# A gap of 96 bytes and one column buffer fewer, ahead of the weight buffers in on-chip memory

## The chip, the cores and the metric

The kernel runs as one program on one core of a Trainium2 chip. The metric is the device time of one execution in microseconds (us): 1457.18 us is the median of three runs, which lie between 1455.75 and 1457.39 us.

## The reference

One sequence of 256 tokens of width 1024 passes seven sublayers in float32: a gated feed-forward (SwiGLU, inner width 2816), an mLSTM mixer, two feed-forwards, a Mamba-2 mixer, a feed-forward, and a hybrid layer (attention of 8 heads beside a gated short convolution). Around each of the first six stands

```
hmod = rms_norm(x, g_pre) * (1 + scale) + shift
y    = rms_norm(fn(hmod), g_post)
x    = x + weight * gate * y
```

`shift`, `scale` and `gate` come from a vector `c` through large matrices (`ada_w`, `w_ada_2`). Nearly all the time is matrix products of the 256 tokens with about 330 MB of float32 weights, each read once.

## The kernel before

**Split weights.** TensorE multiplies in a shorter float32 form (fp32r), so each operand is split into a high part and the rest: `hi` is the weight rounded to fp32r, `lo` is `raw - hi`. A product then takes three matmuls: high by high, high by low, low by high. The activations are split in the same way (`XH`, `XL` for the normalised input; `gh`, `gl` for the inner activations of a feed-forward and the mixers; `AH`, `AL`, `CH`, `CL`, `MH`, `ML` in the hybrid layer).

**The stream.** Class `Stream` (lines 111 to 262) loads the weights in units of 128 rows by 1024 floats, 4096 bytes in each row: a load by SyncE into one of nine `raw` buffers, a cast to `hi` on ScalarE (ACT) or VectorE (DVE), and a subtraction to `lo` on DVE. There are six `hi` and six `lo` buffers. Units that multiply the vector `c` go from `raw` straight into the sums `accC` and `accG` (`mac`, line 366).

**Two roles in a matmul.** TensorE (PE) loads one operand as weights in its array (the stationary operand, 128 columns here) and streams the other through it (the moving operand). In `proj_t` (line 681) the stationary operand is a 128-column piece of `hi` or `lo`, and `XH` or `XL` moves with 256 columns (all the tokens). In `unit_b` and `unit_wide` (lines 709 and 755) it is the other way about: 128 tokens of `XH`, `XL`, `gh` or `gl` are stationary, and 512 columns of `hi` or `lo` move. The profile names the moving operand first: `pa<-XH,hi` moves `XH`, `py<-hi,gh` moves `hi`. The last unit or two of a feed-forward, and the last of the mLSTM, have buffers of their own in the stage's pool (`house`, line 124; `hix`, `lox` in the profile), but are used in the same way and beside the others.

**Order.** The order on every engine is fixed when the program is built, by the `Stream` and a small model of the engines' clocks (`Clock`, `Meter`). It doesn't look at addresses.

**Places in memory.** Pools are laid out one behind another in each row (partition) of the on-chip memory, and each tile begins at the next multiple of 32 bytes. The pool `cst` stands first; in it lie `X`, `XH`, `XL`, small constants, the bf16 scratch `junk`, then the column buffers `AB` (shift and scale of a sublayer as columns, 64 bytes each, line 408) and two buffers `G`. Behind it come `raw`, `hi`, `lo`, `scr`, the small tiles, `accC` and `accG`, and the pools that the stages open and close. In bytes modulo 128, before the change:

| tiles | start |
|---|---|
| `X`, `XH`, `XL` | 0 |
| `G`, all `raw`, `hi`, `lo`, `scr` | 32 |
| `accC`, `accG` | 64 |
| tiles of the first feed-forward (`gf`, `gh`, `gl`, `hix`, `lox`) | 32 |
| `gh`, `gl`, `hix`, `lox` of the mLSTM | 0 |
| the same in the other three feed-forwards; the Mamba-2 tiles; `AH`, `AL`, `CH`, `CL`, `MH`, `ML` | 64 |

The pieces that matmuls take from these tiles begin at multiples of 512 bytes within them, so they have the same value modulo 128.

Of the kernel before, what the change touches and what calls it, by code (L numbers as in the profile page):

```python
# [10 lines left out]
F32 = mybir.dt.float32  # L11
# [254 lines left out]
def tile_blocks(ctx: ExitStack, tc, x, c, ada_w, ada_b, norm_pre, norm_post, ffn_w1, ffn_w3, ffn_w2,  # L266
# [8 lines left out]
    cst = ctx.enter_context(tc.tile_pool(name="cst", bufs=1))  # L275
# [22 lines left out]
    isel = cst.tile([128, 32], F32R, name="isel")  # L298
    cs = cst.tile([128, 16], F32, name="cs")
    junk = cst.tile([128, 512], mybir.dt.bfloat16, name="junk")  # L300

    def pa(shape):
        return psum.tile(shape, F32, name="pa")
# [94 lines left out]
    Gs, ABs = {}, {}  # L398
# [4 lines left out]
    def cols_set(n, p, hs=(0, 1)):  # L403

        v = lambda t: t.rearrange("p (i h) -> p i h", h=2)
        g = colT[:, 16 + 8 * n:24 + 8 * n] if n < 6 else colT[:, 64:72]
        if n not in ABs:
            ABs[n] = cst.tile([128, 16], F32, name="AB", bufs=3)
        for j, h in enumerate(hs):
            if h:  # L410
                V.scalar_tensor_tensor(v(ABs[n][:, 0:8]), p[:, 4 * j:4 * j + 4], 1.0, v(g), op0=OP.add, op1=OP.mult)
            else:
                V.tensor_copy(v(ABs[n][:, 8:16]), p[:, 4 * j:4 * j + 4])

    def ada_cols(n, hs):

        p = side[0]([128, 512])
        us = st.take(len(hs))
        for i in range(8 * len(hs)):
            h, j = i // 8, 4 * (i // 8) + i % 4  # L420
            w = st.get(us[h])[i // 4 % 2]
            T.matmul(p[0:8, 0:256], pick[:, 7 - j:15 - j], w[:, 0, 256 * (i % 4):256 * (i % 4) + 256],
                     start=(i == 0), stop=(i == 8 * len(hs) - 1))
            if i % 8 == 7:
                st.done(us[h])
        r = small.tile([8, 256], F32, name="rows", bufs=1)
        A.copy(r, p[0:8, 0:256])

        def columns():
            q = side[0]([128, 512])  # L430
            for i in range(2):
                T.transpose(q[:, 8 * i:8 * i + 8], r[:, 128 * i:128 * i + 128], ident[:8, :8])
            cols_set(n, q[:, 0:16].rearrange("p (h i) -> p i h", h=2), hs)

        later(3, lambda: safe.append(columns))
# [1177 lines left out]
    with tc.tile_pool(name="pst", bufs=1, space=PSUM) as pst:  # L1613
# [53 lines left out]
        for j in range(16):  # L1667
            cols_sum(p, j)
        pieces("A", 2)
        cols_set(0, p[:, 0:16].rearrange("p (i h) -> p i h", h=2))  # L1670
        affine(tr, 0, 0, "A", True)
        affine(tr, 0, 1, "V")
# [76 lines left out]
```

## Time and profile before

| what | value |
|---|---|
| median of three runs | 1457.18 us |
| the profiled execution | 1456.93 us |
| its span, first to last instruction | 1455.1 us |
| TensorE busy | 1414.0 us, 9482 matmuls |
| VectorE busy | 1225.1 us |
| ScalarE busy | 631.6 us |
| loads and stores | 338.86 MB, mean 233 GB/s |

The span stands 1.8 us below the time of its own execution. Matmuls overlap one another: the duration of one (some 280 ns with 256 columns) is longer than the distance from its start to the next start (some 118 ns), and it is that distance that adds up to the time. It is read from the starts of a row of matmuls, or as the length of a piece of the chain of waits over its count.

### The profile page before, as it was taken

To read this page: it belongs to the slowest core of one execution; us is meant where nothing else is said; L and a number is where in the kernel's file an instruction comes from. 1 tells how busy PE (TensorE), PEld (TensorE's weight loads), DVE (VectorE), ACT (ScalarE), POOL (GpSimd) and SP (SyncE) were. 2 spreads that over 40 slices of the span, in tenths; PEclk is the share of its full clock that TensorE was granted. 3 is DMA by queue.
4 is the path that set the end of the run, shared out by engine and by line. 5 is a ranking of instruction groups with operands and counts; after the bars stand their busy time and mean duration, and the time that the engine had idled before them with its cause. 6 is when DMAs were issued, how large, how long until landed. Compare 5 with 4: busy or idle time off the path is not lost.

```text
span 1455.1 us, 24247 instructions
## 1 busy us (share of the span) xinstructions
PE 1414.0 (97%) x9482; PEld 1281.3 (88%) x9482; DVE 1225.1 (84%) x1755; ACT 631.6 (43%) x1139; POOL 37.9 (3%) x52
## 2 busy tenths in 40 slices
PE   4999999999999999999999999999999999999997
PEld 2899988977999988999889977789998799999996
DVE  7889878978989889888899999887888866879675
ACT  4433336367433354233465876552235613523112
POOL 2000000000000000000100000000000000000000
PEclk9999999999999999999999999999999999999999
DMA  9889955864998867879656444567888664456550
GB/s 376 311 303 357 325 187 194 270 236 158 338 331 314 321 213 250 309 271 319 216 177 174 131 131 131 159 231 231 308 300 286 223 188 131 147 190 201 174 174 30
DMA packets 144011, 338.86 MB, mean 233 GB/s; under 512 B 11496, under 2 KB 23320, under 8 KB 143768
## 3 DMA queue, kind: packets, MB, share of 16 engines
q1 hardware_dynamic: 142088, 332.25, 67.0%
q0 software_dynamic: 1552, 4.81, 0.9%
q8 instruction: 74, 1.21, 0.3%
q14 instruction: 41, 0.34, 0.1%
q10 hardware_dynamic: 256, 0.25, 0.0%
HBM read 334.64 MB, written 2.62 MB: 232 GB/s over the span
## 4 chain that ended last, share of the span: by engine, by line
PE 85%; DVE 7%; ACT 5%; issue 2%; DMA 1%; POOL 0%; ACTq 0%; DVEq 0%; POOLq 0%
PE pa L107 65%; PE py L107 19%; DVE scr L107 2%; ACT junk L107 2%; DVE lo L107 1%; PE cp L107 1%; ACT scr L107 1%; DMA raw<-in_ffn_w_dram 1%; DVE X L107 0%; ACT hi L107 0%; DVE accC L107 0%; ACT L107 0%; DVE XS L107 0%; ACT ss L107 0%; DVE E L107 0%
## 5 line engine op out<-in xcount | busy, mean ns | idle before, releaser
L107 DVE TENSOR_TENSOR lo<-raw,hi 128x1024 fp32r<-128x1024 f32 x450 | 542.2, 1222 | 41.9 <-ACT hi L107 29.3
L107 PE MATMUL pa<-XH,hi 128*128 128x256 f32 x2000 | 566.8, 283 | 1.0 <-ACT tmp L107 1.0
L107 PE MATMUL pa<-XL,hi 128*128 128x256 f32 x2000 | 561.8, 281 | 0.0
L107 PE MATMUL pa<-XH,lo 128*128 128x256 f32 x2000 | 561.7, 281 | 0.0
L107 PEld LDWEIGHTS pa<-XH,hi 128*128 128x128 f32 x2000 | 376.8, 188 | 3.3 <-ACT tmp L107 1.2
L107 PEld LDWEIGHTS pa<-XL,hi 128*128 128x128 f32 x2000 | 377.0, 188 | 1.5 <-issue 0.5
L107 PEld LDWEIGHTS pa<-XH,lo 128*128 128x128 f32 x2000 | 376.8, 188 | 0.0
L107 ACT CAST hi<-raw 128x1024 fp32r<-128x1024 f32 x270 | 275.9, 1050 | 175.1 <-PE pa L107 104.5
L107 DVE SCALAR_TENSOR_TENSOR accC<-raw,cs,accC 128x1024 f32<-128x1024 f32 x112 | 140.2, 1279 | 7.2 <-DMA accC<-in_ada_b_dram 7.1
L107 DVE CAST hi<-raw 128x1024 fp32r<-128x1024 f32 x180 | 124.1, 690 | 16.5 <-PE pa L107 16.2
L107 PE MATMUL pa<-hi,XH 128*128 128x512 f32 x320 | 125.9, 407 | 2.0 <-ACT junk L107 1.1
L107 PE MATMUL pa<-lo,XH 128*128 128x512 f32 x304 | 118.9, 398 | 0.0
L107 PE MATMUL py<-lo,gh 128*128 128x512 f32 x352 | 111.8, 396 | 0.0
L107 PE MATMUL py<-hi,gh 128*128 128x512 f32 x352 | 111.3, 397 | 0.0
L107 PE MATMUL py<-hi,gl 128*128 128x512 f32 x352 | 110.6, 395 | 0.0
L107 PE MATMUL pa<-hi,XL 128*128 128x512 f32 x320 | 96.5, 402 | 2.6 <-DVE ss L107 1.2
L107 ACT ACTIVATE sil<-pa 128x256 f32<-128x256 f32 (+1 forms) x80 | 32.3, 405 | 131.4 <-PE pa L107 131.4
L107 ACT CAST gh<-gf 128x256 fp32r<-128x256 f32 x72 | 28.0, 407 | 125.0 <-DVE gf L107 125.0
L107 PEld LDWEIGHTS py<-lo,gh 128*128 128x128 f32 x352 | 66.2, 188 | 15.7
L107 PEld LDWEIGHTS py<-hi,gl 128*128 128x128 f32 x352 | 66.2, 188 | 15.6
L107 DVE TENSOR_TENSOR gf<-pa,sil 128x256 f32<-128x256 f32 (+1 forms) x80 | 34.3, 447 | 50.7 <-PE pa L107 50.6
L107 PEld LDWEIGHTS py<-hi,gh 128*128 128x128 f32 x352 | 64.5, 188 | 13.9
(306 smaller groups left out, 1568.8 us busy)
## 6 DMA issues: line engine op xcount, KB each, us to landing
raw<-in_ffn_w_dram SPq DMA_DIRECT2D x264, 512.0 KB, 5.4
raw<-in_ada_w_dram SPq DMA_DIRECT2D x144, 512.0 KB, 5.3
raw<-in_w_in_dram SPq DMA_DIRECT2D x80, 512.0 KB, 3.9
raw<-in_mb_w_in_dram SPq DMA_DIRECT2D x41, 512.0 KB, 3.8
raw<-in_ml_w_in_dram SPq DMA_DIRECT2D x25, 512.0 KB, 5.1
raw<-in_w_ada_dram SPq DMA_DIRECT2D x24, 512.0 KB, 5.3
raw<-in_mb_w_out_dram SPq DMA_DIRECT2D x16, 512.0 KB, 4.2
raw<-in_ml_w_out_dram SPq DMA_DIRECT2D x8, 512.0 KB, 5.9
```

What stands on the lines that cost most here:

```text
L107: return fn(out, *args, **kw)
```

## The change

The pool `cst` gets a tile of 24 floats (96 bytes) between `junk` and the column buffers, which nothing reads or writes, and there are two column buffers instead of three (128 bytes instead of 192). All that lies behind begins 32 bytes later. Modulo 128, `G`, `raw`, `hi`, `lo` and `scr` go from 32 to 64, the tiles of the first feed-forward from 32 to 64, those of the mLSTM from 0 to 32, and all that stood at 64 goes to 96. `X`, `XH` and `XL` stay at 0. No instruction is added, removed or moved on any engine, and every instruction waits for the same semaphore values as before.

```
     junk = cst.tile([128, 512], mybir.dt.bfloat16, name="junk")
+    cst.tile([128, 24], F32, name="gap")
...
         if n not in ABs:
-            ABs[n] = cst.tile([128, 16], F32, name="AB", bufs=3)
+            ABs[n] = cst.tile([128, 16], F32, name="AB", bufs=2)
```

## Rows read from the trace of the kernel before

**Rows 1.** The page, parts 1 and 2: busy time; slices of the span
```profile
PE 1414.0 (97%) x9482; PEld 1281.3 (88%) x9482; DVE 1225.1 (84%) x1755; ACT 631.6 (43%) x1139; POOL 37.9 (3%) x52
...
PEclk9999999999999999999999999999999999999999
```
**Rows 2.** The page, part 4: the chain that ended last
```profile
PE 85%; DVE 7%; ACT 5%; issue 2%; DMA 1%; POOL 0%; ACTq 0%; DVEq 0%; POOLq 0%
PE pa L107 65%; PE py L107 19%; DVE scr L107 2%; ACT junk L107 2%; DVE lo L107 1%; PE cp L107 1%; ACT scr L107 1%; DMA raw<-in_ffn_w_dram 1%; DVE X L107 0%; ACT hi L107 0%; DVE accC L107 0%; ACT L107 0%; DVE XS L107 0%; ACT ss L107 0%; DVE E L107 0%
```
**Rows 3.** Busy time by stretches (us) in the second feed-forward; PEclk, DMA share, GB/s
```profile
393.51:404.71 11.20, 11.20 (x51) 9.02 (x50) 11.20 (x15) 5.70 (x7) 0.00 (x0) 1.00 0.80 276
404.71:427.43 22.72, 22.72 (x194) 22.72 (x193) 17.69 (x18) 6.85 (x11) 1.98 (x3) 1.00 0.97 368
```
**Rows 4.** Chain of waits in order of time: start us, us, what
```profile
393.51 11.20 PE py L107 x48
404.71 22.72 PE pa L107 x192
...
1273.48 151.31 PE pa L107 x1284
```
**Rows 5.** Groups of instructions by line and form: PE
```profile
L107 PE MATMUL pa<-XH,hi 128*128 128x256 f32 x2000 | 566.8, 283 | 1.0 <-ACT tmp L107 1.0
...
L107 PE MATMUL pa<-hi,XH 128*128 128x512 f32 x320 | 125.9, 407 | 2.0 <-ACT junk L107 1.1 <-ACT XH L107 0.9
...
L107 PE MATMUL pa<-lo,XH 128*128 128x512 f32 x304 | 118.9, 398 | 0.0
L107 PE MATMUL py<-lo,gh 128*128 128x512 f32 x352 | 111.8, 396 | 0.0
...
L107 PE MATMUL pa<-AH,hi 128*128 128x256 f32 x64 | 17.9, 279 | 0.0
...
L107 PE MATMUL py<-lo,MH 128*128 128x512 f32 x32 | 10.9, 395 | 0.0
```
**Rows 6.** Timeline of PE, end of second feed-forward: start us, us, instruction
```profile
530.51 0.39 PE L107 MATMUL py<-hix,gh 128*128 128x512 f32 x1
...
531.87 0.63 PE L107 MATMUL py<-hi,gh 128*128 128x512 f32 x2
...
533.27 0.63 PE L107 MATMUL py<-hi,gh 128*128 128x512 f32 x2
```
**Rows 7.** Timeline of PE, end of the mLSTM
```profile
335.79 0.39 PE L107 MATMUL py<-hix,gh 128*128 128x512 f32 x1
...
337.16 0.63 PE L107 MATMUL py<-hi,gh 128*128 128x512 f32 x2
...
338.56 0.39 PE L107 MATMUL py<-hi,gh 128*128 128x512 f32 x1
```
**Rows 8.** Timeline of PE, end of the first feed-forward
```profile
222.09 0.39 PE L107 MATMUL py<-hix,gh 128*128 128x512 f32 x1
...
223.48 0.62 PE L107 MATMUL py<-hi,gh 128*128 128x512 f32 x2
...
224.86 0.64 PE L107 MATMUL py<-hi,gh 128*128 128x512 f32 x2
```
**Rows 9.** Timeline of PE in the hybrid layer
```profile
1369.00 0.28 PE L107 MATMUL pa<-CH,hi 128*128 128x256 f32 x1
...
1371.80 0.28 PE L107 MATMUL pa<-CH,hi 128*128 128x256 f32 x1
```
**Rows 10.** Timeline of PE where 8 columns are stationary
```profile
204.86 0.62 PE L107 MATMUL pa<-hi,pick 128*8 128x256 f32 x4
...
206.24 0.63 PE L107 MATMUL pa<-lo,pick 128*8 128x256 f32 x4
```
**Rows 11.** Groups of DVE, 66 to 212 us and 375 to 540 us
```profile
L107 DVE TENSOR_TENSOR gl<-gf,gh 128x256 fp32r<-128x256 f32 x16 | 5.9, 417 | 0.0
...
L107 DVE TENSOR_TENSOR gl<-gf,gh 128x256 fp32r<-128x256 f32 x18 | 6.8, 419 | 0.1
```

## What the change will do: the prediction

> **What bounds the kernel now.** I read the page's busy times first: PE is busy 1414.0 of 1455.1 us, DVE 1225.1 [rows 1]. A busy PE might still wait for others, so the chain of waits comes next: PE has 85% of it, 65% in matmuls that write `pa` and 19% in those that write `py` [rows 2]. The busy time by stretches shows the same inside a feed-forward: PE has no gap in 393.51 to 427.43 us, at full granted clock, while DVE is busy 11.20 of 11.20 us in the `py` stretch and 17.69 of 22.72 us in the `pa` stretch [rows 3]. So the time is the number of matmuls times the distance between their starts, and DVE, with 85% of that group, is the next bound.
>
> The distances come from the chain. 48 `py` matmuls with 512 columns take 11.20 us, 233.3 ns each; 192 `pa` matmuls with 256 columns take 22.72 us, 118.3 ns each [rows 4]. They hold on to these values through the whole kernel.
>
> **Whether a start matters.** The change issues no instruction and shifts addresses only, so I looked for places where before already has the same matmul at another start. The ends of the stages are such places: there `hix` and `lox` move instead of `hi` and `lo`, with the same shape, the same stationary tiles, one right behind the other.
> - Second feed-forward: six matmuls with `hix`, `lox` at 64 modulo 128 take 530.51 to 531.87, 1.36 us, 226.7 ns each. The next six, with `hi`, `lo` at 32, take 1.40 us, 233.3 ns each [rows 6].
> - mLSTM: `hix`, `lox` at 0 take 1.37 us for six, the next six at 32 take 1.40 us [rows 7].
> - First feed-forward: here `hix`, `lox` stand at 32 as `hi` and `lo` do, and the two sixes take 1.39 and 1.38 us [rows 8].
>
> So a moving operand of 512 columns that begins at a multiple of 64 goes 6.6 ns faster (2.8%) than one at 32 past it, and where both stand at 32 the difference is gone. The stationary tile matters less: `gh` at 64, 0 and 32 under the same moving `hi` gives 233.3, 233.3 and 230 ns [rows 6 to 8].
>
> The page "SBUF — State Buffer" of the Trainium skill (section Door 1) says that consecutive accesses within 16-byte lines run at full bandwidth; by it a start at 32 is as good as one at 64, and the time would stay at 1457. The rows speak against it: 226.7 beside 233.3 ns. That rule is rival D.
>
> **The sum.** All against the profiled execution, 1456.93 us, which is 0.25 us below the median.
> 1. Moving `hi` and `lo` go from 32 to 64. Their matmuls: 320 of `hi` by `XH`, as many by `XL`, 304 of `lo` by `XH`, three groups of 352 by `gh` and `gl`, three of 32 by `MH` and `ML` [rows 5], and 140 in smaller groups: 2236 by 6.6 ns, 14.8 us less.
> 2. `hix` and `lox` go the other way in four stages (64 to 96, 0 to 32): 84 matmuls by 6.6 ns, 0.5 us more; the 12 of the first feed-forward gain 0.1.
> 3. `AH`, `AL`, `CH`, `CL` move with 256 columns in six groups of 64 [rows 5], and go from 64 to 96. No row shows 256 columns at both starts. Bounds: nothing, or 6.6 ns as with 512. I take half, 3.3 ns for half the columns: 384 by 3.3 ns, 1.3 us more (0 to 2.5). The 96 matmuls that move `hi` by `pick` gain 0.3 by the same measure.
> 4. The 6000 matmuls that move `XH` or `XL` (three groups of 2000 [rows 5]) keep their moving start at 0; only their stationary `hi` or `lo` goes from 32 to 64. I take zero, by the rows on `gh` above. The other ends: half of 226.7 ns is 113.3, so at best 5.0 ns less each, 30 us; at worst 3.3 ns more each, 20 us.
> 5. DVE and ACT read and write the same tiles. `gl` from `gf` and `gh` takes 417 ns where all three stand at 32 and 419 ns where they stand at 64 [rows 11]: zero.
> 6. The loads write `raw` at 64 instead of 32. DMA holds 1% of the chain [rows 2], 15 us; a packet 3% slower or faster would move it by 0.5 us. Zero.
> 7. Two column buffers: a buffer is rewritten two sublayers after its last reading, and no wait differs from before. Zero.
>
> Lines 1 to 3 give 13.3 us. PE's own idle time is 41 us of the span, and in the `py` stretches DVE has no slack [rows 3], so some of the gain is lost again in waits for `lo`; I pass on nine tenths: 12.0 us. 1456.93 - 12.0 = 1444.9, forecast **1445**. Its own range is 1437 to 1451: if DVE held back all of the gain in the matmuls by `gh` and `gl` (1056 by 6.6 ns, 7.0 us), 1451 would be left; if the stationary start were worth 1.4 ns to the 6000 (8.4 us, by 0.9), 1437.
>
> Of step 4 there is more to say, since it is the largest unknown. 118.3 ns is 5 ns over half of 226.7, with a moving operand that begins at 0. Something costs these 5 ns, and the stationary `hi` at 32 is one candidate. The other is the load of the weights itself, which with 256 columns has half the time to hide in. With only 8 stationary columns (`pick`) and a moving `hi` at 32, twelve matmuls take 1.38 us, 115 ns [rows 10]: less than 118.3 in spite of the worse start, so the weight load costs something as such. And `CH` at 64 over the same `hi` at 32 takes 2.80 us for 24, 116.7 ns [rows 9], so a mere shift of the moving start by 64 is worth 1.6 ns.
>
> The page "TensorE: Matmul & The Clock Gate" of the Trainium skill (part 2, the weight-load step) gives PE two independent read ports, one for the moving operand and one for the weights, so that a load takes nothing from the running matmul. By it the stationary start can't matter and step 4 is zero; that hangs together with the `gh` rows, but not with `pick`, whose small load is quicker.
>
> **The rivals.**
> - B: any operand off a multiple of 64, moving or stationary, costs the slow pace. Then the 6000 fall to 113.3 ns: 30.0 us less. In exchange the matmuls by `gh`, `gl`, `MH`, `ML` outside the first feed-forward (about 900, stationary now at 96 or 32) gain nothing: 5.9 us back. 13.3 + 30.0 - 5.9 = 37.4, of which I pass on eight tenths since DVE is then near its limit all through: 1427. For it: the unexplained 5 ns. Against it: the `gh` rows.
> - B': the 6000 fall to the 116.7 ns that `CH` shows: 9.8 us more, (13.3 + 9.8) by 0.9 is 21 us: 1436. For it: the offset between the two operands becomes 64 in size where it was 32. Against: nothing says that the offset is what distinguishes `CH`.
> - C, slower: with `XH` at 0 and `hi` at 64 both reads of a 256-column matmul begin on a multiple of 64 and get into each other's way, 3.3 ns each time (the upper end of step 4): 20 us by 0.9 more, 1456.9 - 12.0 + 18 = 1463. The place is every `proj_t` in the feed-forwards and the hybrid layer; it outweighs the gain from 2.0 ns a matmul up (12.0 us over 6000). For it: 118.3 and 116.7 ns show that the pairing of starts has some effect. Against: `hix` by `gh`, at 64 and 64 and at 0 and 0, is the fastest pair in the trace.
> - D, no change: `hix` is fast for another reason than its start, for example because it is alone in its buffers while `hi` rotates through six. Then 1457. Against it: the first feed-forward, whose `hix` is just as alone and as slow as `hi` [rows 8].
>
> **Chances and range.** Forecast 0.55, B' 0.14, B 0.12, C 0.10, D 0.09. What a measurement of this kernel can tell from no change is about 0.2%, 2.9 us. Faster: forecast, B' and B, 0.81; same: D, 0.09; slower: C, 0.10. The range leaves out C and the lower half of B: 1425 to 1458.
>
> **What the profile after would show.** Right: a piece of 48 `py` matmuls in the chain takes 10.9 us instead of 11.20, and one of 192 `pa` still 22.7 us; `hix` is now slower than `hi` at the end of the second feed-forward; DVE's groups keep their means; DVE's share of the span rises to 85%, with more waits of PE for `lo`. B shows 21.8 us for the 192, with `py` hardly faster outside the first feed-forward; B' 22.4; C over 23.1. The forecast is wrong in its ground if the 48 `py` still take 11.20 us, and wrong in its passing on if they take 10.9 and the span falls by less than 8 us.

## The result, and the profile after

The changed kernel takes 1434.2 us (median of 4 runs, 1431.8 to 1435.8); the kernel before took 1457.2 us beside it. The ratio is 0.9845, with a 95% interval of 0.9832 to 0.9858: 23 us faster. The forecast was 1445 us. The profiled execution after took 1431.77 us, with a span of 1430.0 us. All times leave out three executions, one of them the profiled one of the kernel with a gap of 160 bytes (whose trace is therefore not used), that took between 2.3 and 6.4 ms.

The page after, busy times and the chain of waits by engine (before: [rows 1, 2]):

```profile
PE 1388.1 (97%) x9482; PEld 1258.6 (88%) x9482; DVE 1223.5 (86%) x1755; ACT 631.6 (44%) x1139; POOL 37.9 (3%) x52
...
PE 82%; DVE 10%; ACT 4%; issue 2%; DMA 1%; ACTq 0%; SPq 0%; DVEq 0%
```
PE is busy 25.9 us less, the span is 25.1 us shorter, DVE's work is the same within 2 us. So PE's matmuls became quicker and nearly all of it was passed on. Which matmuls, the chain of waits in the second feed-forward tells (start us, us, what; before: [rows 4]):

```profile
389.17 11.19 PE py L107 x48
400.36 21.77 PE pa L107 x192
```
48 `py` took 11.20 us and take 11.19. 192 `pa` took 22.72 us and take 21.77: from 118.3 to 113.4 ns each. That is the reverse of what I had forecast. The groups of PE say the same for the whole span (busy, mean ns of one; before: [rows 5]):

```profile
L107 PE MATMUL pa<-XH,hi 128*128 128x256 f32 x2000 | 559.0, 280 | 1.3 <-ACT tmp L107 1.1 <-DVE y L107 0.3
...
L107 PE MATMUL pa<-hi,XH 128*128 128x512 f32 x320 | 124.8, 403 | 2.0 <-ACT junk L107 1.1 <-ACT XH L107 0.9
...
L107 PE MATMUL pa<-lo,XH 128*128 128x512 f32 x304 | 117.8, 394 | 0.0
L107 PE MATMUL py<-lo,gh 128*128 128x512 f32 x352 | 111.8, 396 | 0.0
...
L107 PE MATMUL pa<-AH,hi 128*128 128x256 f32 x64 | 17.9, 279 | 0.0
```
Every pair of `XH` or `XL` with `hi` or `lo` is quicker, whichever of the two moves (means of 283, 407 and 398 ns became 280, 403 and 394). `hi` and `lo` over `gh` (396) and `AH` over `hi` (279) are as before. DVE has its old load in both stretches (us; busy PE, PEld, DVE, ...; before: [rows 3]):

```profile
389.17:400.36 11.19, 11.19 (x50) 9.02 (x50) 11.19 (x15) 5.70 (x7) 0.00 (x0) 1.00 0.83 288
400.36:422.13 21.77, 21.77 (x193) 21.77 (x193) 17.70 (x18) 6.81 (x11) 1.98 (x3) 1.00 1.01 388
```

The trace holds one more thing. In the first feed-forward the `pa` stretches stayed near the old pace (chain of waits after; before they took 22.72 us):

```profile
129.46 22.61 PE pa L107 x192
152.07 11.13 PE py L107 x48
163.20 22.61 PE pa L107 x192
```
22.61 us for 192 is 117.8 ns each, and every matmul of such a stretch has this pace. Over the whole span about 80% of the `XH`, `XL` matmuls run at 113 to 114 ns and the rest near 118, in whole stretches but for the first few matmuls of some; the mean is 114.3 ns.

### The profile page after: what moved, and what is told of

Its sections match the earlier page's. It is cut to its first block, busy times and chain, and to the rows that moved or that the text cites. A ratio compares the mean times of both kernels' runs of the same rounds, so it can differ in the third digit from the quotient of the medians.

```text
span 1430.0 us, 24247 instructions
## 1 busy us (share of the span) xinstructions
PE 1388.1 (97%) x9482; PEld 1258.6 (88%) x9482; DVE 1223.5 (86%) x1755; ACT 631.6 (44%) x1139; POOL 37.9 (3%) x52
## 4 chain that ended last, share of the span: by engine, by line
PE 82%; DVE 10%; ACT 4%; issue 2%; DMA 1%; ACTq 0%; SPq 0%; DVEq 0%
PE pa L107 61%; PE py L107 19%; DVE scr L107 3%; DVE lo L107 3%; ACT junk L107 2%; PE cp L107 1%; ACT scr L107 1%; PE pb L107 1%; DMA oh<-in_consts_dram 1%; DVE hi L107 1%; DVE XS L107 1%; DMA raw<-in_mb_w_in_dram 1%; DVE X L107 0%; DVE E L107 0%; ACT L107 0%
## 5 line engine op out<-in xcount | busy, mean ns | idle before, releaser
L107 DVE TENSOR_TENSOR lo<-raw,hi 128x1024 fp32r<-128x1024 f32 x450 | 542.1, 1222 | 36.2 <-ACT hi L107 23.7
L107 PE MATMUL pa<-XH,hi 128*128 128x256 f32 x2000 | 559.0, 280 | 1.3 <-ACT tmp L107 1.1
L107 PE MATMUL pa<-XL,hi 128*128 128x256 f32 x2000 | 554.0, 277 | 0.0
L107 PE MATMUL pa<-XH,lo 128*128 128x256 f32 x2000 | 554.0, 277 | 0.0
L107 PE MATMUL pa<-lo,XH 128*128 128x512 f32 x304 | 117.8, 394 | 0.0
L107 PEld LDWEIGHTS pa<-hi,XL 128*128 128x128 f32 x320 | 59.2, 189 | 18.3 <-DVE XL L107 5.0
```

Source lines behind the costliest of these rows:

```text
L107: return fn(out, *args, **kw)
```

## The experiments

All kernels are the kernel before with other gaps of unused bytes or, once, with two column buffers; none issues another instruction. Below, D is where the moving tile of a matmul begins minus where its stationary tile begins, modulo 256. The slices that one matmul reads begin at multiples of 512 bytes within their tiles, so D is the same for all matmuls of a pair of tiles. Addresses are those that the build assigned; paces are mean distances from one matmul's start to the next in the traces.

**The change halved: the gap alone.**
```diff
+    cst.tile([128, 8], F32, name="gap")      # behind junk; AB keeps bufs=3
```


> One half of the change alone: three column buffers as before, and a gap of 32 bytes, so that hi, lo and all behind them stand where the whole change puts them (hi, lo at 64 modulo 128, XH, XL at 0). Theory R (what counts is the difference of the two starts, moving minus stationary, modulo 64; where it is 0 a matmul is fast, where it is 32 it is slow): same as with the whole change, 1434 us (1431 to 1437), 192 pa matmuls in about 21.8 us, 48 py in 11.20. Theory B (what counts is each operand's own start: off a multiple of 64 is slow): the same, since no start differs. Rival N (the third column buffer itself takes part in it, by the waits for its release): between 1440 and 1457.

Measured: 1431.2 us, ratio 0.9829 (0.9816 to 0.9843), beside 0.9845 (0.9832 to 0.9858) for the whole change. The second feed-forward reads as after the change:
```profile
399.02 21.77 PE pa L107 x192
```
The gap alone gives the whole gain: the two intervals overlap, and no effect of the number of column buffers shows beyond the bytes that it frees. N falls.

**The buffers alone.**
```diff
-            ABs[n] = cst.tile([128, 16], F32, name="AB", bufs=3)
+            ABs[n] = cst.tile([128, 16], F32, name="AB", bufs=2)
```


> The other half alone: two column buffers and no gap. hi, lo move by 64 bytes, from 32 to 96 modulo 128; the difference to XH, XL stays 32 modulo 64. R and B: as before, 1457 us (1454 to 1460), 192 pa in 22.7 us, 48 py in 11.20. N: some of the gain, 1434 to 1450. If the start modulo 128 and not modulo 64 counted, 192 pa would leave 22.7 us.

Measured: 1448.8 us, ratio 0.9951 (0.9937 to 0.9965): faster by 8 us, where R and B had no change.
```profile
390.64 11.20 PE py L107 x48
401.84 22.40 PE pa L107 x192
```
A shift of `hi`, and of all that lies behind it, by 64 bytes took the 192 from 22.72 to 22.40 us. Whatever the rule is, it doesn't repeat after 64 bytes.

**Both operands off a multiple of 64.**
```diff
+    cst.tile([128, 8], F32, name="gapx")     # ahead of X
+    cst.tile([128, 8], F32, name="gap")      # behind junk
```


> X, XH, XL (and the small constants behind them) moved by 32 bytes, hi and lo by 64 in all: XH, XL at 32 and hi, lo at 96 modulo 128, so neither begins at a multiple of 64, and their difference is 0 modulo 64. The stage tiles (gh, AH, CH, MH) stay at 32 from hi. R: 192 pa in about 21.8 us, 256-column matmuls of XH by hi at 113 to 115 ns, py unchanged at 11.20 for 48; 1434 us (1430 to 1438). B: both operands are now off, so all stay slow: 118.3 ns or more, 22.7 us for 192, 1457 us or more.

Measured: 1432.0 us, ratio 0.9836 (0.9820 to 0.9852).
```profile
398.95 21.77 PE pa L107 x192
```
With `XH` at 32 and `hi` at 96 the pace is that of 0 and 64, to the hundredth of a us. Moving both operands by 32 leaves the pace as it is: the difference counts, and not either start. B, and the ground of my forecast with it, falls.

**The stage tiles moved by 32.**
```diff
+    small.tile([128, 8], F32, name="gaps", bufs=1)   # ahead of accs
+    rc.tile([128, 8], F32, name="gapr")              # first in the pool "start"
```


> The kernel before with the stage tiles (gh, gl, hix, AH, CH, MH and the rest) moved by 32 bytes and nothing else: hi, lo stay at 32 modulo 128, gh comes to 96 or 32, so their difference becomes 0 modulo 64 outside the first feed-forward (where it is 0 before and after). XH by hi stays at 32 apart. R: 48 py in 10.9 us (226.7 ns each) instead of 11.20, AH and CH over hi at 113.4 instead of 116.7 ns, 192 pa unchanged at 22.7; about 900 by 6.6 ns and 384 by 3.3 ns are 7.2 us, of which DVE, full in the py stretches, may hold back some: 1451 us (1449 to 1456). B: gh, AH, CH now stand off a multiple of 64, so nothing is gained and some may be lost: 1457 to 1461 us, py 11.20 or more.

Measured: 1455.7 us, ratio 0.9995 (0.9986 to 1.0004): nothing. But the trace has two answers. The first feed-forward in the chain of the kernel before:
```profile
120.47 11.14 PE py L107 x48
```
The first and the second feed-forward in this kernel (the second before: [rows 4]):
```profile
120.58 10.99 PE py L107 x48
...
392.93 11.19 PE py L107 x48
```
In the second, where D became 192 (a multiple of 64, as R asks), `py` stayed. In the first, where D went from 128 to 64, it fell from 11.14 to 10.99. R falls here: being a multiple of 64 apart isn't enough. A few pairs apart (listed under the table below), the paces so far fit one table by D modulo 256, and D of 64 is also what `hi` by `XH` has after the change. That was the next theory, R256.

**`hi` further on, three times.** Only the size of the gap behind `junk` changes (96, 160, 224 bytes: 24, 40, 56 elements), and the stage tiles move along.
```diff
+    cst.tile([128, 24], F32, name="gap")     # 40 and 56 in the other two
```


> Three column buffers and a gap of 96 bytes: hi, lo at 0 modulo 128, as XH and XL; the stage tiles move along with hi. Theory R (the difference of the two starts modulo 64 decides, here 0): as the whole change, 1434 us (1430 to 1438), 192 pa in 21.8 us. Theory R256 (the difference counts modulo 256; D is the moving start minus the stationary one): for hi by XH D is 128, which in the first feed-forward and the mLSTM (hi by gh) went with 232.3 ns; for XH by hi D is 128 too, with 256 columns in no run so far, so between 113.4 and 118.3 ns: 1432 to 1457 us.

> Three column buffers and a gap of 160 bytes: hi, lo begin at 64 modulo 128 and XH, XL at 0, word for word as after the change, but 128 bytes further on; the stage tiles move along. R, and any rule on starts modulo 128: 1434 us (1430 to 1438), 192 pa in 21.8 us. R256: D is 64 for XH by hi, where AH and CH over hi took 117.8 ns, and 192 for hi by XH, where hi by gh took 233.2 ns: 192 pa in 22.6 us, 1453 us (1449 to 1458).

> Three column buffers and a gap of 224 bytes: hi, lo and XH, XL begin at the same place modulo 256 (D is 0 both ways); the stage tiles move along with hi. R256: D of 0 went with 226.7 ns for hix by gh, so hi by XH takes 226.7 to 229 ns, and XH by hi half of it, 113.4 ns: 1432 us (1428 to 1436). R: hi at 96 and XH at 0 modulo 128 are 32 apart modulo 64? No: the start of hi is 128 modulo 256, as XH's, so the difference is 0 modulo 64 too and R gives 1434 as well. A theory by which the two operands, beginning at the same place, get in each other's way would give 1457 or more.

Measured: 96 bytes 1459.5 us, ratio 1.0023 (1.0013 to 1.0034); 160 bytes 1450.2, 0.9958 (0.9942 to 0.9975); 224 bytes 1462.5, 1.0042 (1.0027 to 1.0057). The time with 160 bytes is that of three runs (1448.9 to 1451.1). The chain of the other two, 96 and then 224:
```profile
405.37 22.78 PE pa L107 x192
```
```profile
404.90 23.02 PE pa L107 x192
```
The kernel with 160 bytes is the plainest: `hi` at 64 modulo 128 and `XH` at 0, as the change's own description has it, and 16 us slower than the change. Modulo 64 or 128 nothing holds; R is done with. Of R256 the form stands, two of its sizes don't: at D of 128 `XH` by `hi` takes 118.9 ns in the mean, just above the upper bound, and at D of 0 it takes 119.9 where I expected 113.4, half of what 512 columns take. With 512 columns D of 0 is quick all the same (228.0 ns for `hi` by `XH`). The two widths have tables of their own.

**`gh` level with `hi`.**
```diff
+    cst.tile([128, 8], F32, name="gap")
+    small.tile([128, 56], F32, name="gaps", bufs=1)
+    rc.tile([128, 40], F32, name="gapr")
```


> The gap of 32 bytes (hi, XH as after the change) and the stage tiles 224 bytes further (160 more in the first feed-forward), so that gh, gl, AH, CH and MH begin at the same place modulo 256 as hi (D is 0; in the mLSTM 192). R256: 48 py in 10.9 to 11.0 us outside the mLSTM (226.7 to 229 ns each) instead of 11.20, AH and CH over hi 113.4 instead of 116.7 ns; about 950 by 5 ns and 384 by 3.3 ns are 6 us, of which DVE, full in the py stretches, may hold back up to all: 1428 us (1424 to 1433). R: the same, since D is 0 modulo 64. If py stays at 11.20 us, something other than the offset of the two tiles sets it.

Measured: 1434.9 us, ratio 0.9858 (0.9841 to 0.9874): no better than the change, and above the expected 1424 to 1433.
```profile
387.65 10.92 PE py L107 x48
398.57 22.61 PE pa L107 x192
```
`py` gained what R256 gave it, 11.19 to 10.92 us. But the `pa` stretch behind it, with its D unchanged, now runs at 117.8 ns. So at D of 192 `XH` by `hi` has two paces, and a stretch keeps to one. Over the span 46% are quick here, 80% after the change. `AH` and `CH` over `hi`, now at D of 0, went from 116.7 to 119.8 ns where I expected 113.4; `XH` by `hi` has 119.9 at that D (224 bytes).

**`gh` 64 bytes off `hi`.** After the change the stretches right behind `hi` by `XH` (D 64) and behind `py` at D of 224 were quick, those behind `py` at 128 slow.
```diff
+    cst.tile([128, 8], F32, name="gap")
+    small.tile([128, 40], F32, name="gaps", bufs=1)
+    rc.tile([128, 40], F32, name="gapr")
```


> As e9_py0, but the stage tiles 64 bytes less far (gaps of 32 ahead of the weights, 160 ahead of the stage tiles, 160 in the first feed-forward), so that hi begins 64 past gh, gl, AH, CH and MH modulo 256, as it does past XH (D is 64 for hi by gh, 192 for AH and CH over hi; 0 in the mLSTM). Theory R256 with modes (the pace follows D; at D of 192 XH by hi runs a whole stretch at either 113.4 or 117.7 ns, by what preceded it: fast behind D of 64 or 224, slow behind 0 or 128): 48 py in 11.0 us (229 ns each, 1036 by 4 ns is 4 us), AH and CH over hi at 113.4 to 114 ns (1.1 us), and the 432 XH matmuls behind py in the first feed-forward at 113.4 instead of 117.7 (1.8 us), so 1432.5 less 7: 1426 us (1423 to 1430). Rival (the slow mode comes with any faster py, since PE then outruns what prepares its operands): the slow share of XH by hi rises as in e9_py0, 1432 to 1436 us.

Measured: 1426.7 us, ratio 0.9797 (0.9783 to 0.9812).
```profile
387.06 10.98 PE py L107 x48
398.05 21.79 PE pa L107 x192
```
`py` and `pa` are quick together, and `CH` and `CL` over `hi` and `lo`, at D of 192, take twelve rounds of three matmuls in 4.08 us, 113.3 ns each (timeline of PE in the hybrid layer):
```profile
1339.78 0.28 PE L107 MATMUL pa<-CH,hi 128*128 128x256 f32 x1
...
1343.86 0.28 PE L107 MATMUL pa<-CH,hi 128*128 128x256 f32 x1
```
The rival (a faster `py` as such brings the slow pace) falls. One part failed: in the first feed-forward the slow pace stayed, behind `py` at D of 64 (chain of waits):
```profile
116.92 11.01 PE py L107 x48
127.93 22.61 PE pa L107 x192
```

**The two offsets left, to close the table** (gaps of 64 and 128 bytes).
```diff
+    cst.tile([128, 16], F32, name="gap")     # 32 in the other
```


> Three column buffers and a gap of 64 bytes: hi stands 96 past XH modulo 256, D is 96 for hi by XH and 160 for XH by hi (with 256 columns in no run so far); the stage tiles move along. R256: hi by XH 233.3 ns as E shows at 96; XH by hi open between 113.4 and 119.9 ns, the rows on both sides (128: 118.9, 192: 114.3 in the mean) make 117 likely: 1450 us (1430 to 1462). A rule modulo 64 (32 apart): 1457, 118.3 ns.

> Three column buffers and a gap of 128 bytes: hi begins at 32 modulo 128 exactly as in the kernel before, only 128 bytes further; the stage tiles move along. D is 160 for hi by XH (234.1 ns where hi by gh has it) and 96 for XH by hi (256 columns, in no run so far; its neighbours 64 and 128 took 117.8 and 118.9 ns). R256: 1457 us (1452 to 1463), with a mean for XH by hi that differs from 118.3. A rule modulo 64 or 128: exactly as before, 1457 us, 118.3 and 233.3 ns.

Measured: 64 bytes 1457.8 us, ratio 1.0009 (1.0000 to 1.0019); 128 bytes 1465.5, 1.0068 (1.0052 to 1.0085). The chain of the one and of the other:
```profile
403.34 22.79 PE pa L107 x192
```
```profile
405.17 23.04 PE pa L107 x192
```
For the first I had taken 117 ns as likely, and it is 118.4 in the mean. The second puts `hi` where it was modulo 128, and is 10 us slower than before: no rule modulo 128 allows that. It is also above the 1452 to 1463 that I gave, since `XH` by `hi` at D of 96 takes 120.0 ns.

**What sets the pace that is kept.** The kernel with `gh` 64 off, without its gap in the first feed-forward:
```diff
-    rc.tile([128, 40], F32, name="gapr")
```


> As e10_py64 without the extra 160 bytes in the first feed-forward: there hi begins 224 past gh modulo 256 instead of 64 past it (D of 224 for hi by gh, as in the second to fifth feed-forward after the change). It asks what leaves XH by hi at the slow 117.7 ns in the first feed-forward (two stretches of 192 and one of 48). If it is the D of the py matmuls ahead of them: 224 was followed by the fast 113.4 ns in nine stretches out of nine after the change, so the three stretches come to 21.8 us for 192; 432 by 4.3 ns less, 250 py by 4.2 ns more, 1425.9 us. If it is the place (the first feed-forward, whatever the offset): 117.7 ns stays, 22.6 us for 192, and py at 233.3 ns costs 1.0 us: 1427.7 us.

Measured: 1425.0 us, ratio 0.9787 (0.9773 to 0.9800), the lowest median of all, though its interval overlaps that of the kernel before it. The decision lies in the trace of the first feed-forward:
```profile
118.65 11.19 PE py L107 x48
129.84 21.78 PE pa L107 x192
```
`py` is slower there and all three stretches behind it are quick, at the same place in the program where they were slow. So the place doesn't decide; what differs ahead of these stretches is the D of `py`, and with it the pace that a stretch takes. `py` at D of 224 led to the quick one in 12 stretches of 12 that followed without a pause (9 after the change, 3 here), at D of 0 and 128 to the slow one in 15 of 15 (12 with `gh` level, 3 after the change). At D of 64 it led to either (quick in 9 of 12 with three gaps), and after a pause, or right behind the few matmuls by `pick`, both occur; what decides there is open.

The paces in the traces, in ns per matmul. The moving tile is named first; a value is the mean over the three kinds of matmul that alternate in a stretch. "Or" stands where stretches of the same D settle at one of two paces:

| D | 256 columns: `XH`, `XL`, `AH`, `AL`, `CH`, `CL` by `hi`, `lo` | 512 columns: `hi`, `lo` by `XH`, `XL`, `gh`, `gl`, `MH`, `ML` |
|---|---|---|
| 0 | 119.9 | 226.9 to 228.0 |
| 32 | 116.7, or 117.8 | 233.2 to 233.3 |
| 64 | 117.8 | 228.9 to 229.6 |
| 96 | 120.0 | 233.4 |
| 128 | 118.6, or 120.0 | 232.3 to 232.7 |
| 160 | 117.3, or 118.7 | 234.0 to 234.2 |
| 192 | 113.4, or 117.8 | 233.3 |
| 224 | 118.3 | 233.1 to 233.3 |

So D of 192 isn't alone in having two paces. At D of 128, with a gap of 96 bytes, the two stretches of 192 behind `py` at D of 128 take 120.0 ns, and those behind `py` at 224 take 118.6. That the count goes by 256 and not by 512 shows at D of 192: the full distance is 192 past a multiple of 512 for `AH` by `hi` with three gaps (113.3 ns) and 448 past one for `XH` by `hi` (113.4).

No kernel was built for one rival: that PE's reads collide with those of DVE and ACT, or with the loads, which use the same tiles, and not with one another. The traces speak against it: the paces are the same where VectorE, ScalarE and GpSimd rest and no DMA packet is under way. There `CH`, `CL` by `hi`, `lo` take 116.7 ns before (D of 32), 120.0 with `gh` level (D of 0) and 113.3 with three gaps (D of 192), from 45 to 50 matmuls each; `hi`, `lo` by `MH`, `ML` take 233.3, 226.7 and 228.9 (D of 224, 0 and 64), from 20 or 21 each.

Not all pairs keep to the table: `hi` by `E` takes 233.3 at D of 64, `hi` by `scr` 231 at 0, and `hix` by `gh`, in groups of twelve, 227 to 232 at 0.

## Why the prediction was right in sign and wrong in its ground

The sign held, and 1434.2 us lies in the range of 1425 to 1458; but that range took in everything from B's 1427 to no change. The forecast's own range, 1437 to 1451, was missed, and the gain was twice the forecast, 23 us against 12. That the time came out faster was mostly luck: of the 14.8 us of step 1 only 3.6 came, and nearly all of the gain came from step 4, which I had put at zero.

- **Step 1 failed.** It gave 2236 matmuls 6.6 ns each for the moving start, 14.8 us. Some 940 of them (by `XH`, `XL`) gained 3.8 ns (233.2 to 229.4), 3.6 us; the 1056 by `gh` and `gl` and the 96 by `MH` and `ML` gained nothing. I had compared `hix` by `gh` with `hi` by `gh` [rows 6, 7] and put the difference down to where `hix` begins. But `hix` lies in the same pool as `gh`, at D of 0, and `hi` at 224 or 160: what differed was the pair. My control, the first feed-forward [rows 8], has D of 0 and 128 and was one of the exceptions: there `hix` is slow at D of 0, for a reason that no run shows. The sentence that the forecast is wrong in its ground if 48 `py` still take 11.20 us has come true.
- **Step 2 failed with it.** `hix` went to 96, off a multiple of 64, with D still 0, and was not slower than `hi`. Timeline after, end of the second feed-forward: six in 1.40 us (the old pace of `hi`) and then `hix` by `gh`, the next three starts in 0.69 us, 230 ns each:
```profile
531.27 0.63 PE L107 MATMUL py<-hix,gh 128*128 128x512 f32 x2
...
532.67 0.39 PE L107 MATMUL py<-hix,gh 128*128 128x512 f32 x1
...
533.36 0.39 PE L107 MATMUL py<-hix,gh 128*128 128x512 f32 x1
```
- **Step 3**: the 384 by `AH` and the others did not move (116.7 before and after); D is 32 in both.
- **Step 4 was the mis-sized term**: 6000 matmuls costed at zero, with 30 us less as one end. They fell by 4.0 ns in the mean (118.3 to 114.3), 24 us: nearly all of the gain. I took zero from the rows on `gh`, where the stationary start had changed and the pace hardly, and these had changed D between values that cost the same (224, 160) or nearly (128). The `pick` rows [rows 10] don't tell the cost of a weight load either: its pieces stand at D of 164 to 192, another distance than that of `XH` by `hi` (224).
- **Steps 5 to 7** held: `lo` from `raw` and `hi` takes 1222 ns in both, DMA 1% of the chain, and the gap alone gives the whole gain.
- **The passing on** was nine tenths, as I took it: the gains in pace add up to 27.6 us (24 and 3.6), and the span fell by 25.1.
- **The rivals.** B foretold the signs (192 in 21.8 us, `py` as before) and 1427 us; a fifth of the matmuls keep the slow pace, which cost 5 us. Its ground, each operand's own start, is refuted by the kernel with both at 32 off; that `AH` over `hi` stayed was in keeping with it. B' came nearest in time, 1436, and its ground, the offset between the two operands, was the right kind; but it took the size of the offset alone and put the 192 at 22.4 us, the pace of `CH`, where they took 21.77. C's mechanism, two operands that begin level and cost more, exists at D of 0 (119.9 ns), not where the change puts `hi`. D, no change, is out.

The error was one of inference: three observations of a pair of addresses were read as a rule on one of them. Two rows could have raised the doubt: `gh` at 32 under the same `hi` gave 230 and not 233.3 ns [rows 8], and `CH` and `XH` over the same `hi` gave 116.7 and 118.3 [rows 9, 4]. I used the first to clear the stationary operand, and read the second as a moving start, instead of asking about the difference.

## What to carry to other kernels

Where PE's chain has matmuls end to end, compute the distance of start to start for every pair of operands and list it against the difference of the two tiles' addresses before anything else: a gap of 32 bytes was worth 1.7% here, and two gaps 2.1%. Change one gap at a time, and look at each stage apart, since one pair's gain can put the next pair at a slower pace (the kernel with `gh` level with `hi`). The offsets found here are this kernel's: weights that begin 64 bytes past the activations modulo 256, which is D of 64 where the weights move with 512 columns and D of 192 where the activations move with 256. A new tile in an early pool shifts them all.

## What the runs showed of the hardware

- The distance between fp32r matmuls depended on the difference of the two operands' starts modulo 256, and not on either start where both were moved by 32: 113.4 to 120.0 ns with 256 columns, 227 to 234 ns with 512, a few pairs excepted (`hi` by `E`, by `scr`, and `hix` by `gh`). `hi` 128 bytes further on, equal modulo 128, costs 16 us from the change's place (1450.2 beside 1434.2) and 10 from that of before.
- The Trainium skill's page "TensorE: Matmul & The Clock Gate" (part 2, the weight-load step) has the operands read through two independent ports, so that loading the next weights takes nothing from the running matmul. The runs speak against it: 113.3 or 120.0 ns for the same matmul (`CH` by `hi`, D of 192 or 0), with the other engines and the loads at rest, is hard to have if the two reads never meet. That they meet is inferred, and how was not measured.
- At D of 192 a stretch of 256-column matmuls settles within its first few at 113.4 or at 117.8 ns and keeps to it; behind `py` at D of 224 it was the quick one in 12 of 12, behind 0 and 128 the slow one in 15 of 15. A change of one pair's offset can so move the time of the pair behind it, by 0.83 us for 192 matmuls.
